# Folded score triangles and a three-operation rotary in a two-layer hybrid decoder kernel

## The chip, the cores and the metric

One core of a Trainium2 chip runs the whole program. Its engines work beside each other, each through its own instructions in order: TensorE (PE: matmuls and transposes into PSUM), VectorE (DVE), ScalarE (ACT), GpSimd (POOL) and the DMA queues, issued by SyncE (SP). The metric is the device time of one execution in microseconds; the median of several runs is compared.

## The reference, cut to what matters

Each of two layers normalises x, projects it to queries, keys, values and pooling channels, mixes tokens, projects back, and runs a SwiGLU network. All of it is float32. What the change touches is partial rotary and the sliding-window attention with sinks: 1024 positions, 8 query heads on 2 key heads of 64 channels, blocks of 128 positions, a window of 128.

```python
def partial_rotary(t, positions):          # first 16 of 64 channels of each head
    t1, t2, rest = tf[..., :half], tf[..., half:ROT_DIM], tf[..., ROT_DIM:]
    rot = jnp.concatenate([t1 * cos - t2 * sin, t2 * cos + t1 * sin, rest], axis=-1)
...
    scores = scores * (HEAD_DIM ** -0.5)   # queries of a block x (block before, own block)
    diff = qi + BLOCK - kj
    valid = (diff[None] >= 0) & (diff[None] < WINDOW) & (key_abs >= 0)
    scores = jnp.where(valid[None, :, None, None], scores, NEG_INF)
    probs = jax.nn.softmax(jnp.concatenate([scores, sink], axis=-1), axis=-1)[..., :-1]
    out = jnp.einsum("bnkgqs,bnskd->bnqkgd", probs.astype(v.dtype), v_cat)
```

With the window as wide as a block, query i of a block sees the keys j <= i of its own block and the keys j > i of the block before: two triangles that fill one 128 x 128 square between them.

## The kernel before

Every float32 product is computed as three matmuls (`mm3`, lines 263, 266, 267) on operands split into a high and a low part: ScalarE casts the high part (L220), VectorE subtracts it from the source (L221). Positions are worked in two halves of 512. For each layer and half, dense projections accumulate in four PSUM banks, and a weight's split is asked for one step ahead.

Attention is a generator of steps (`attention`, L940) that advances beside the dense steps (`run`, L693): 37 attention steps beside 20 dense steps for half 0 (L1490); for half 1, 16 beside the output projection of half 0 (L1496), 10 beside the pooling projection (L1521), and the rest beside the first gate/up products (L1525). A group is one block and one key head with its four query heads: 8 groups a half, 32 over both layers. Its steps are: rotary and keys (for the first key head of a block) and queries; softmax of the group before; scores of two heads and probabilities of the group before; the same for the other two heads. A group's value products are issued one step after its probabilities were transposed.

The generators set priorities; a scheduler at build time then orders each engine's instructions by priority and readiness, so that dense matmuls and attention matmuls mix on TensorE.

In a group, `att_scores` (L858) multiplies into one PSUM bank for two heads, [head, block before | own block]; VectorE adds the mask, takes the maximum and writes to SBUF (L869). `att_softmax` (L876) makes exponentials with a sum (L888), adds the sink's, and scales three heads on VectorE (L894) and one on ScalarE (L896). `att_probs` (L898) transposes 4 tiles for two heads (L904) and splits them (L220, L221); `att_values` (L913) multiplies 256 columns at a time. In block 0 there is no block before, and the tiles are half as wide. `att_rotary` (L787) has six VectorE instructions of 80 elements per block. Its tables are made at the start (L196 to L206) by a chain of small VectorE instructions.

Of the kernel before, what the change touches and what calls it, by code (L numbers as in the profile page):

```python
# [11 lines left out]
F32 = mybir.dt.float32  # L12
F32R = mybir.dt.float32r
# [7 lines left out]
P = 128  # L21
# [45 lines left out]
def hybrid_decoder_kernel(  # L67
# [70 lines left out]
    def msc_bank():  # L138
# [19 lines left out]
    pick_row = t_("rt", [P, 7])  # L158
# [29 lines left out]
    cos_t = const.tile([P, NB, RH], F32, name="cos_t")  # L188
    sin_t = const.tile([P, NB, RH], F32, name="sin_t")
# [5 lines left out]
    def rotary_angles():  # L195
# [591 lines left out]
    def att_rotary(blk, qkv):  # L787
        rot = qkv[:, 0:QK].rearrange("p (n d) -> p n d", d=HD)
        t1 = rot[:, :, 0:RH]
        t2 = rot[:, :, RH:ROT]  # L790
        nr = NH + NKV
        cb = cos_t[:, blk : blk + 1, :].to_broadcast([P, nr, RH])
        sbc = sin_t[:, blk : blk + 1, :].to_broadcast([P, nr, RH])
        tmp = t_("rt", [P, 4, nr, RH])
        nc.vector.tensor_mul(tmp[:, 0], t1, cb)
        nc.vector.tensor_mul(tmp[:, 1], t2, sbc)
        nc.vector.tensor_mul(tmp[:, 2], t2, cb)
        nc.vector.tensor_mul(tmp[:, 3], t1, sbc)
        nc.vector.tensor_sub(t1, tmp[:, 0], tmp[:, 1])
        nc.vector.tensor_add(t2, tmp[:, 2], tmp[:, 3])  # L800
# [57 lines left out]
    def att_scores(blk, n, u, qT, mx, s):  # L858

        kT = attn["k", blk]  # L860
        bank = msc_bank()
        cs = att_seen(blk)
        for ii in range(2):
            dst = bank[:, ii * 2 * P : (ii + 1) * 2 * P][:, cs]
            q = qT[:, (2 * u + ii) * P : (2 * u + ii + 1) * P]
            nc.tensor.matmul(dst, q, kT[:, 2 * n, cs], start=True, stop=False)
            nc.tensor.matmul(dst, q, kT[:, 2 * n + 1, cs], start=False, stop=True)
        for ii in range(2):
            nc.vector.tensor_tensor_reduce(  # L869
                out=s[:, ii, cs], in0=bank[:, ii * 2 * P : (ii + 1) * 2 * P][:, cs],  # L870
                in1=mask[:, cs], scale=SCALE, scalar=-3.0e38, op0=ALU.add, op1=ALU.max,
                accum_out=mx[:, 2 * u + ii : 2 * u + ii + 1],
            )
        return s

    def att_softmax(blk, n, sts, mx, nsink):  # L876
        hs = slice(n * GRP, (n + 1) * GRP)
        nm = t_("st", [P, 8])[:, :GRP]
        es = t_("st", [P, 8])[:, :GRP]
        sm = t_("st", [P, 8])[:, :GRP]  # L880
        nc.vector.scalar_tensor_tensor(
            nm, mx[:, :GRP], -1.0, nsink[:, hs], op0=ALU.mult, op1=ALU.min
        )
        nc.vector.tensor_sub(es, nm, nsink[:, hs])
        nc.scalar.activation(es, es, AF.Exp)
        for i in range(GRP):
            sl = sts[i // 2][:, i % 2, att_seen(blk)]
            nc.scalar.activation(sl, sl, AF.Exp, bias=nm[:, i : i + 1], accum_out=sm[:, i : i + 1])  # L888
        nc.vector.tensor_add(es, es, sm)
        nc.vector.reciprocal(es, es)  # L890
        for i in range(GRP):
            sl = sts[i // 2][:, i % 2, att_seen(blk)]
            if i < GRP - 1:
                nc.vector.tensor_scalar(sl, sl, es[:, i : i + 1], None, op0=ALU.mult)  # L894
            else:
                nc.scalar.activation(sl, sl, AF.Copy, scale=es[:, i : i + 1])  # L896

    def att_probs(blk, s):  # L898

        bank = msc_bank()  # L900
        for ck in range(0 if blk else 1, 2):
            for ii in range(2):
                i = 2 * ck + ii
                nc.tensor.transpose(  # L904
                    bank[:, i * P : (i + 1) * P], s[:, ii, ck * P : (ck + 1) * P], ident
                )
        ph = t_("pth", [P, 512], F32R)
        pl = t_("ph", [P, 512], F32R)
        cs = slice(0 if blk else 2 * P, 4 * P)
        split(ph[:, cs], pl[:, cs], bank[:, cs])  # L910
        return ph, pl

    def att_values(blk, n, u, probs, cat, t):  # L913
# [747 lines left out]
```

## Time and profile before

| | us |
|---|---|
| runs, median of 3 | 1906.67 |
| lowest, highest | 1903.42, 1907.11 |
| the profiled execution, first to last instruction (span) | 1904.4 |
| TensorE, VectorE, ScalarE, GpSimd busy in it | 1864.7, 1540.4, 948.4, 20.0 |

The profile gives the span as the profiled execution's own time; it lies 2.3 us under the median and inside the runs' range. Matmuls are pipelined: the record of a 512-column matmul lasts 0.39 us while the next one starts 0.227 us after it, so "busy" of TensorE says that work is in flight, and the distance between two starts says what an instruction costs. An idle time stands in brackets with the instruction that ended it.

### The profile page before, as it was taken

The page shows a single profiled execution, that of the slowest core. Times are in us where ns is not written, and L with a number is a line of the kernel's source. Part 1 is how long each engine was busy: PE and PEld are TensorE (multiplying, and loading weights), DVE is VectorE, ACT ScalarE, POOL GpSimd, SP SyncE. Part 2 cuts the span into 40 slices and gives each one's busy share as a digit, 9 for nine tenths or more (in the row PEclk, how much of TensorE's full clock was granted, in tenths as well). Part 3 has the DMA queues.
Part 4 walks back from the last instruction along what each step waited for, and adds up shares of the span by engine and source line. Part 5 has one row for each costly group of instructions (what it writes and reads, how often), then busy time and mean ns, then how long its engine had stood idle before and what let it go on. Part 6 is the DMA issues. An engine that isn't in the chain of part 4 may idle for free.

```text
span 1904.4 us, 26019 instructions
## 1 busy us (share of the span) xinstructions
PE 1864.7 (98%) x8954; PEld 1540.3 (81%) x8954; DVE 1540.4 (81%) x2889; ACT 948.4 (50%) x1791; POOL 20.0 (1%) x67
## 2 busy tenths in 40 slices
PE   7999999999999999999999999999999999999998
PEld 5887788888888788888888868888887888888886
DVE  7899886668898888788879988846888888867687
ACT  4875795654222223445558667845622222234452
POOL 0000000000000000000000000000000000000000
PEclk9999999999999999999999989999999999999999
DMA  9345563655555665944554464536654565574343
GB/s 341 112 144 161 161 221 125 191 172 193 194 183 188 205 210 172 320 143 150 172 179 139 126 181 164 178 111 209 214 189 146 198 216 197 199 249 157 117 141 114
DMA packets 229540, 341.86 MB, mean 180 GB/s; under 512 B 17016, under 2 KB 126472, under 8 KB 229408
## 3 DMA queue, kind: packets, MB, share of 16 engines
q1 hardware_dynamic: 228800, 338.10, 53.8%
q10 hardware_dynamic: 576, 2.10, 0.3%
q8 instruction: 70, 1.15, 0.3%
q14 instruction: 62, 0.51, 0.1%
q0 software_dynamic: 32, 0.00, 0.0%
HBM read 267.25 MB, written 72.89 MB: 179 GB/s over the span
## 4 chain that ended last, share of the span: by engine, by line
PE 80%; DVE 10%; DMA 5%; ACT 3%; issue 2%; SPq 0%; DVEq 0%; ACTq 0%; POOL 0%; POOLq 0%
PE acc L263 25%; PE acc L266 24%; PE acc L267 24%; DMA ar<-in_ada_w_dram 2%; DVE lo L221 1%; DVE ada L298 1%; DMA raw<-in_w_up_dram 1%; PE msc L904 1%; PE msc L561 1%; ACT hi L220 1%; PE pv L263 1%; PE pv L266 1%; PE pv L267 1%; ACT raw L554 1%; DVE fn L1162 1%
## 5 line engine op out<-in xcount | busy, mean ns | idle before, releaser
L220 ACT ACTIVATE hi<-raw 128x1024 fp32r<-128x1024 f32 (+1 forms) x388 | 331.8, 868 | 360.1 <-PE acc L266 197.1
L221 DVE TENSOR_TENSOR lo<-raw,hi 128x1024 fp32r<-128x1024 f32 (+1 forms) x388 | 380.2, 987 | 121.3 <-ACT hi L220 116.4
L263 PE MATMUL acc<-t,hi 128*128 128x512 f32 x704 | 274.6, 390 | 2.7 <-ACT hi L220 2.6
L266 PE MATMUL acc<-t,hi 128*128 128x512 f32 x704 | 274.0, 389 | 0.0
L267 PE MATMUL acc<-t,lo 128*128 128x512 f32 x704 | 271.8, 389 | 0.0
L263 PE MATMUL acc<-bh,hi 128*128 128x512 f32 x520 | 202.8, 390 | 0.0
L267 PE MATMUL acc<-bh,lo 128*128 128x512 f32 x520 | 202.4, 389 | 0.0
L263 PE MATMUL acc<-hT,hi 128*128 128x512 f32 x480 | 190.2, 396 | 0.6 <-DVE fn L691 0.6
L266 PE MATMUL acc<-hT,hi 128*128 128x512 f32 x480 | 188.4, 392 | 0.0
L267 PE MATMUL acc<-hT,lo 128*128 128x512 f32 x480 | 187.6, 392 | 0.0
L1162 DVE TENSOR_TENSOR fn<-acc,fn 128x512 f32<-128x512 f32 x220 | 150.3, 685 | 38.2 <-PE acc L267 37.6
L263 PEld LDWEIGHTS acc<-t,hi 128*128 128x128 f32 x704 | 132.2, 188 | 32.1 <-ACT hi L220 5.1
L267 PEld LDWEIGHTS acc<-t,lo 128*128 128x128 f32 x704 | 132.2, 188 | 28.7 <-DVE lo L221 1.2
L266 PEld LDWEIGHTS acc<-t,hi 128*128 128x128 f32 x704 | 132.2, 188 | 27.1
L266 PE MATMUL acc<-ph,hi 128*128 128x512 f32 x320 | 124.7, 390 | 0.0
L1098 ACT ACTIVATE fn<-fn 128x512 f32<-128x512 f32 x44 | 27.9, 633 | 181.7 <-DVE fn L1162 181.7
L263 PEld LDWEIGHTS acc<-bh,hi 128*128 128x128 f32 x520 | 97.6, 188 | 20.2
L267 PEld LDWEIGHTS acc<-bh,lo 128*128 128x128 f32 x520 | 97.6, 188 | 20.2
L298 DVE SCALAR_TENSOR_TENSOR ada<-ar,c_act,ada 128x512 f32<-128x512 f32 x140 | 104.6, 747 | 10.1 <-DMA ar<-in_ada_w_dram 9.7
L263 PE MATMUL acc<-hi 128*128 128x512 f32 x256 | 103.5, 410 | 2.4 <-DVE fn L691 2.0
L263 PEld LDWEIGHTS acc<-hT,hi 128*128 128x128 f32 x480 | 90.2, 188 | 19.2 <-DVE fn L691 1.4
L267 PEld LDWEIGHTS acc<-hT,lo 128*128 128x128 f32 x480 | 90.1, 188 | 18.6 <-issue 0.2
(323 smaller groups left out, 3814.5 us busy)
## 6 DMA issues: line engine op xcount, KB each, us to landing
ar<-in_ada_w_dram SPq DMA_DIRECT2D x160, 256.0 KB
raw<-in_w_gate_dram SPq DMA_DIRECT2D x44, 512.0 KB
raw<-in_w_up_dram SPq DMA_DIRECT2D x44, 512.0 KB
raw<-in_w_in_dram SPq DMA_DIRECT2D x80, 256.0 KB
raw<-keeps SPq DMA_DIRECT2D x40, 512.0 KB
keeps<-fn SPq DMA_DIRECT2D x66, 256.0 KB
two_b<-in_w_down_dram SPq DMA_DIRECT2D x30, 512.0 KB
raw<-keepa SPq DMA_DIRECT2D x25, 512.0 KB
```

Of the source, the lines that this page charges most:

```text
L220: a = nc.scalar.activation(hi, src, AF.Copy)
L221: v = nc.vector.tensor_sub(lo, src, hi.bitcast(F32))
L263: ins = nc.tensor.matmul(dst, lh, rh, start=first, stop=False)
L266: nc.tensor.matmul(dst, lh, rl, start=False, stop=False)
L267: return nc.tensor.matmul(dst, ll, rh, start=False, stop=last)
L298: ins = nc.vector.scalar_tensor_tensor(acc, w, c_act[:, i : i + 1], acc, op0=ALU.mult, op1=ALU.add)
L554: nc.scalar.activation(hf, bank, AF.Identity, bias=shift, scale=scale)
L561: ins = nc.tensor.transpose(bank[:, t * P : (t + 1) * P], src[t], ident)
L904: nc.tensor.transpose(bank[:, i * P : (i + 1) * P], s[:, ii, ck * P : (ck + 1) * P], ident)
L1098: nc.scalar.activation(g, g, AF.Silu)
L1162: nc.vector.tensor_add(halves_of(dst)[m], bank, halves_of(src)[m])
```

## The change

The scores of both triangles are folded into one tile S of [128, 4 heads, 128 + 1]. ScalarE copies the block before from PSUM to S, VectorE copies the own block over it where key j <= query i (a predicated copy with the mask `own`), and the 129th column holds the sink divided by the scale, copied there by GpSimd. One maximum over 129 columns and one negated scaling follow; the exponentials run over 129 columns, and their sum includes the sink. One multiplication scales all four heads. Four transposes and one split per group follow; then GpSimd cuts the triangles apart again, in the transposed tiles: two selects write the own block's part (`here`), two clear it from the other (`seen`). In block 0 GpSimd fills S with a large negative number in place of ScalarE's copy, and there are two selects. Value products take all four heads at once, the own block first; they are issued after the next group's queries, three steps after the transposes. Rotary works on both halves at once, with a table of (-sin, sin) and one of (cos, cos), and its scratch is the rest of S's tile. The mask table becomes 128 wide; `pth` has four buffers in place of two, `st` nine in place of twelve.

```diff
-    SMALL = dict(junk=1, st=12, rs=8, ss=4, halo=8, rows=1, cols=2, colp=4, sk=2)
+    SMALL = dict(junk=1, st=9, rs=8, ss=4, halo=8, rows=1, cols=2, colp=4, sk=2)
-        mix=dict(cfa=2, cfb=2, qkv=5, bqkv=1, uT=4, pt=2, vz=5, rt=1, qT=1, pth=2, pwh=1, pwl=1),
+        mix=dict(cfa=2, cfb=2, qkv=5, bqkv=1, uT=4, pt=2, vz=5, qT=1, pth=4, pwh=1, pwl=1),
...
-    mask = const.tile([P, 2 * P], F32, name="mask")
-    nc.gpsimd.memset(mask, 0.0)
-    fill = NEG / SCALE
+    own = const.tile([P, P], F32, name="own")
+    nc.gpsimd.memset(own, 1.0)
     nc.gpsimd.affine_select(
-        out=mask, in_=mask, pattern=[[-1, 2 * P]], compare_op=ALU.is_ge,
-        fill=fill, base=P, channel_multiplier=1,
-    )
-    nc.gpsimd.affine_select(
-        out=mask, in_=mask, pattern=[[1, 2 * P]], compare_op=ALU.is_gt,
-        fill=fill, base=0, channel_multiplier=-1,
+        out=own, in_=own, pattern=[[-1, P]], compare_op=ALU.is_ge,
+        fill=0.0, base=0, channel_multiplier=1,
     )
...
-    cos_t = const.tile([P, NB, RH], F32, name="cos_t")
-    sin_t = const.tile([P, NB, RH], F32, name="sin_t")
+    cos_t = const.tile([P, NB, ROT], F32, name="cos_t")
+    sin_t = const.tile([P, NB, ROT], F32, name="sin_t")
...
-        nc.vector.tensor_scalar(sin_t, ang, math.pi, -math.pi, op0=ALU.min, op1=ALU.max)
-        nc.vector.scalar_tensor_tensor(cos_t, sin_t, -1.0, sin_t, op0=ALU.mult, op1=ALU.max)
-        nc.vector.tensor_scalar(cos_t, cos_t, -1.0, math.pi / 2.0, op0=ALU.mult, op1=ALU.add)
+        halves = [slice(0, RH), slice(RH, ROT)]
+        up = sin_t[:, :, halves[1]]
+        nc.vector.tensor_scalar(up, ang, math.pi, -math.pi, op0=ALU.min, op1=ALU.max)
+        nc.vector.tensor_scalar(sin_t[:, :, halves[0]], up, -1.0, None, op0=ALU.mult)
+        nc.vector.tensor_tensor(turns, sin_t[:, :, halves[0]], up, op=ALU.max)
+        for half in halves:
+            nc.vector.tensor_scalar(cos_t[:, :, half], turns, -1.0, math.pi / 2.0, op0=ALU.mult, op1=ALU.add)
...
+    def att_rotary(blk, qkv, room):
         rot = qkv[:, 0:QK].rearrange("p (n d) -> p n d", d=HD)
...
+        both = rot[:, :, 0:ROT].rearrange("p n (o d) -> p n o d", o=2)
         nr = NH + NKV
...
+        cb, sbc = (
+            tab[:, blk : blk + 1, :].rearrange("p b (o d) -> p b o d", o=2).to_broadcast([P, nr, 2, RH])
+            for tab in (cos_t, sin_t)
+        )
+        tmp = room[:, : 2 * nr * RH].rearrange("p (n o d) -> p n o d", n=nr, o=2)
+        nc.vector.tensor_mul(tmp, both[:, :, ::-1, :], sbc)
+        nc.vector.tensor_mul(both, both, cb)
+        nc.vector.tensor_add(both, both, tmp)
...
+    def att_scores(blk, u, qT, kT, S):
         bank = msc_bank()
         cs = att_seen(blk)
         for ii in range(2):
             dst = bank[:, ii * 2 * P : (ii + 1) * 2 * P][:, cs]
             q = qT[:, (2 * u + ii) * P : (2 * u + ii + 1) * P]
...
+            nc.tensor.matmul(dst, q, kT[0][:, cs], start=True, stop=False)
+            nc.tensor.matmul(dst, q, kT[1][:, cs], start=False, stop=True)
+        both = bank.rearrange("p (i o k) -> p i o k", i=2, o=2)
+        dst = S[:, 2 * u : 2 * u + 2, 0:P]
+        if blk:
+            nc.scalar.activation(dst, both[:, :, 0, :], AF.Copy)
+        else:
+            nc.gpsimd.memset(dst, NEG)
+        seen = own.bitcast(I32).rearrange("p (o k) -> p o k", o=1).to_broadcast([P, 2, P])
+        nc.vector.copy_predicated(dst, seen, both[:, :, 1, :])
+    def att_max(S):
+        mx = t_("st", [P, 8])[:, :GRP]
+        nc.vector.tensor_reduce(mx, S, axis=mybir.AxisListType.X, op=ALU.max)
+        nc.vector.tensor_scalar(mx, mx, -SCALE, None, op0=ALU.mult)
+        return mx
+    def att_softmax(S, nm):
+        sm = t_("st", [P, 8])[:, :GRP]
+        es = t_("st", [P, 8])[:, :GRP]
+        for i in range(GRP):
+            nc.scalar.activation(
+                S[:, i, :], S[:, i, :], AF.Exp, bias=nm[:, i : i + 1], scale=SCALE, accum_out=sm[:, i : i + 1]
             )
...
+        nc.vector.reciprocal(es, sm)
+        nc.vector.tensor_mul(
+            S[:, :, 0:P], S[:, :, 0:P], es.rearrange("p (i o) -> p i o", o=1).to_broadcast([P, GRP, P])
         )
...
+    def att_probs(blk, S):
+        bank = msc_bank()
         for i in range(GRP):
...
+            nc.tensor.transpose(bank[:, i * P : (i + 1) * P], S[:, i, 0:P], ident)
+        seen = [t_("pth", [P, 512], F32R) for _ in range(2)]
+        split(*seen, bank)
+        views = [r.rearrange("p (i q) -> p i q", i=GRP) for r in seen]
+        if not blk:
+            for v in views:
+                nc.gpsimd.affine_select(
+                    out=v, in_=v, pattern=[[0, GRP], [1, P]], compare_op=ALU.is_ge,
+                    fill=0.0, base=0, channel_multiplier=-1,
                 )
...
+            return [None, seen]
+        here = [t_("pth", [P, 512], F32R) for _ in range(2)]
+        for v, r in zip(views, here):
+            nc.gpsimd.affine_select(
+                out=r.rearrange("p (i q) -> p i q", i=GRP), in_=v, pattern=[[0, GRP], [1, P]],
+                compare_op=ALU.is_ge, fill=0.0, base=0, channel_multiplier=-1,
+            )
+        for v in views:
+            nc.gpsimd.affine_select(
+                out=v, in_=v, pattern=[[0, GRP], [-1, P]], compare_op=ALU.is_gt,
+                fill=0.0, base=0, channel_multiplier=1,
+            )
+        return [seen, here]
+    def att_values(blk, n, probs, cat, t):
+        if n == 0:
             attn["pv"] = ps.tile([P, 512], F32, tag="pv", name="pv", bufs=1)
         pv = attn["pv"]
...
+        for ck in (1, 0) if blk else (1,):
             vh, vl = attn["v", blk - 1 + ck]
             vs = slice(n, n + 2)
...
+            opening = n == 0 and ck == 1
+            closing = n == NKV - 1 and ck == (0 if blk else 1)
             ins = mm3(
...
+                pv, vh[:, vs].rearrange("p a d -> p (a d)"), vl[:, vs].rearrange("p a d -> p (a d)"),
+                *probs[ck], opening, closing, None if opening else attn["open"],
             )
             if opening:
                 attn["open"] = ins
...
+        if n == NKV - 1:
             nc.scalar.activation(
                 cat[:, :, t * P : (t + 1) * P], pv.rearrange("p (j q) -> p j q", j=GRP), AF.Copy
             )
...
+    def attention(h, qkvs, sink, cat):
         NG = NT * NKV
         prev, late = None, []
             if g < NG:
                 t, n = divmod(g, NKV)
                 blk = h * NT + t
+                both = t_("sb", [P, D])
+                S = both[:, : GRP * (P + 1)].rearrange("p (i k) -> p i k", i=GRP)
+                room = both[:, GRP * (P + 1) :]
                 if n == 0:
                     if t == 0:
...
+                        att_rotary(blk, qkvs[t], room)
                     att_keys(blk, qkvs[t])
                     if t + 1 < NT:
...
+                        att_rotary(blk + 1, qkvs[t + 1], room)
                 qT = att_queries(n, qkvs[t])
...
+                hs = slice(n * GRP, (n + 1) * GRP)
+                nc.gpsimd.tensor_copy(S[:, :, P : P + 1], sink[:, hs].rearrange("p (i o) -> p i o", o=1))
                 yield
+            flush()
             if prev:
...
+                att_softmax(prev[3], prev[4])
                 yield
             for u in range(GRP // 2):
+                if cur is None and g < NG:
+                    cur = (blk, n, t, S)
                 if cur:
+                    kT = attn["k", blk]
+                    att_scores(blk, u, qT, (kT[:, 2 * n], kT[:, 2 * n + 1]), S)
+                    if u:
+                        cur = (*cur, att_max(S))
+                if prev and u == 0:
+                    late.append((prev[0], prev[1], att_probs(prev[0], prev[3]), cat, prev[2]))
                 yield
+        nc.vector.tensor_scalar(sk, sk, 1.0 / SCALE, None, op0=ALU.mult)
+        d["bq"], d["sink"] = bq, sk
```

## Rows read from the trace of the kernel before

**Rows 1.** The page's head and first part: busy us, share of the span, instructions.

```profile
span 1904.4 us, 26019 instructions
PE 1864.7 (98%) x8954; PEld 1540.3 (81%) x8954; DVE 1540.4 (81%) x2889; ACT 948.4 (50%) x1791; POOL 20.0 (1%) x67
```

**Rows 2.** Table by stage: busy us (instructions) of each engine, clock, DMA share, GB/s.

```profile
60.00:160.00 100.00, 98.36 (x622) 85.06 (x621) 93.76 (x288) 77.01 (x194) 3.33 (x11) 1.00 0.40 122
160.00:205.00 45.00, 40.38 (x184) 30.72 (x183) 40.31 (x103) 28.02 (x67) 0.28 (x1) 0.92 0.62 180
450.00:500.00 50.00, 50.00 (x222) 41.41 (x221) 39.52 (x51) 11.55 (x13) 0.00 (x0) 1.00 0.52 169
1000.00:1096.00 96.00, 94.36 (x592) 81.27 (x592) 90.40 (x276) 74.29 (x188) 3.59 (x11) 1.00 0.44 133
...
165.40:168.80 3.40, 3.27 (x12) 2.33 (x11) 3.40 (x7) 3.03 (x6) 0.00 (x0) 0.50 0.56 154
1131.40:1138.20 6.80, 6.24 (x13) 4.37 (x14) 6.59 (x19) 3.32 (x11) 0.70 (x1) 0.50 0.59 164
```

**Rows 3.** TensorE's waits over the span: us in total, times, longest.

```profile
PE msc L332 <- DVE ident L152: 11.2, 1, 11.2
PE msc L904 <- DVE sb L894: 2.1, 5, 0.6
PE pv L263 <- ACT pth L220: 1.8, 2, 0.9
```

**Rows 4.** Timeline of TensorE, 263.5 to 268.2 us: start, us, instruction [idle before].

```profile
...
263.89 0.28 PE L267 MATMUL pv<-pth,vz 128*128 128x256 f32 x1
264.01 0.60 PE L904 MATMUL msc<-ident,sb 128*128 128x128 f32 x4
264.45 0.60 PE L561 MATMUL msc<-ident,fn 128*128 128x128 f32 x4
...
266.44 0.39 PE L263 MATMUL pv<-pth,vz 128*128 128x256 f32 x1 [0.92 <-ACT pth L220]
```

**Rows 5.** Groups by line, VectorE: out<-in, shape, xcount, busy, mean ns.

```profile
L869 DVE CUSTOM_DVE_ANT_0 sb<-msc,mask 128x256 f32<-128x256 f32 x112 | 44.2, 416 | 7.8 <-PE msc L867 7.4
L869 DVE DVE_READ_ACCUMULATOR2_ANT st<- 128x1 f32 x128 | 10.4, 82 | 0.0
L894 DVE TENSOR_SCALAR sb<-sb,st 128x256 f32<-128x256 f32 x84 | 24.5, 346 | 0.3
L221 DVE TENSOR_TENSOR ph<-msc,pth 128x512 fp32r<-128x512 f32 x56 | 38.2, 685 | 1.3 <-issue 0.4 <-ACT pth L220 0.4
L881 DVE SCALAR_TENSOR_TENSOR st<-st,sk 128x4 f32<-128x4 f32 x32 | 5.0, 155 | 0.1
L796 DVE TENSOR_TENSOR rt<-qkv,sin_t 128x80 f32<-128x80 f32 x16 | 3.8, 235 | 0.0
```

**Rows 6.** Groups by line, ScalarE.

```profile
L888 ACT ACTIVATE sb<-sb,st 128x256 f32<-128x256 f32 x112 | 55.6, 502 | 5.9 <-DVE st L881 5.9
L888 ACT ACTIVATION_READ_ACCUMULATOR sb<-sb,st 128x1 f32 x128 | 24.7, 193 | 0.0
L220 ACT ACTIVATE pth<-msc 128x512 fp32r<-128x512 f32 x56 | 33.0, 597 | 20.7 <-PE msc L904 20.6
```

**Rows 7.** GpSimd: two groups by line, and its timeline from 955 to 958 us.

```profile
L166 POOL TENSOR_SCALAR_AFFINE_SELECT mask<-mask 128x256 f32<-128x256 f32 x1 | 0.4, 391 | 0.0
masks.py:199 POOL TENSOR_SCALAR_AFFINE_SELECT G<-G 128x128 f32<-128x128 f32 x1 | 0.3, 299 | 0.1
...
955.25 2.24 POOL L808 CAST vz<-vz_zero 128x64 fp32r<-128x64 f32 x4 [680.14 <-ACT hT L220]
957.48 0.23 POOL L808 CAST vz<-vz_zero 128x64 fp32r<-128x64 f32 x1
```

**Rows 8.** Timeline of VectorE, 10.3 to 11.7 us.

```profile
...
10.84 0.20 DVE L206 TENSOR_SCALAR cos_t<-cos_t 128x64 f32<-128x64 f32 x1
10.95 0.22 DVE L152 CAST ident<-G 128x128 fp32r<-128x128 f32 x1
```

More of the change, by code (lines that the diff above doesn't have):

```diff
@@ L157, in hybrid_decoder_kernel @@
     ones = ones_r.bitcast(F32)
-    pick_row = t_("rt", [P, 7])
+    pick_row = t_("pth", [P, 7])
     nc.vector.memset(pick_row, 0.0)
@@ L865, in att_scores @@
             q = qT[:, (2 * u + ii) * P : (2 * u + ii + 1) * P]
[L866 to L872, printed above, removed]
-            )
@@ L874, in att_scores @@
[L874 to L882, printed above, removed]
-        )
-        nc.vector.tensor_sub(es, nm, nsink[:, hs])
-        nc.scalar.activation(es, es, AF.Exp)
+            nc.tensor.matmul(dst, q, kT[0][:, cs], start=True, stop=False)
@@ L886, in att_softmax @@
         for i in range(GRP):
[L887 to L905, printed above, removed]
-                )
[L907 to L911, printed above, removed]
@@ L913, in att_values @@
-    def att_values(blk, n, u, probs, cat, t):
-        if n == 0 and u == 0:
+            nc.tensor.transpose(bank[:, i * P : (i + 1) * P], S[:, i, 0:P], ident)
[7 more added lines that the diff above has]
+                    fill=0.0, base=0, channel_multiplier=-1,
+                )
+            return [None, seen]
@@ L916, in att_values @@
+        return [seen, here]
+    def att_values(blk, n, probs, cat, t):
+        if n == 0:
             attn["pv"] = ps.tile([P, 512], F32, tag="pv", name="pv", bufs=1)
         pv = attn["pv"]
-        ph, pl = probs
-        first = 0 if blk else 1
-        for ck in range(first, 2):
+        for ck in (1, 0) if blk else (1,):
             vh, vl = attn["v", blk - 1 + ck]
             vs = slice(n, n + 2)
-            cs = slice(ck * 2 * P, (ck + 1) * 2 * P)
-            opening = n == 0 and u == 0 and ck == first
-            closing = n == NKV - 1 and u == 1 and ck == 1
+            opening = n == 0 and ck == 1
+            closing = n == NKV - 1 and ck == (0 if blk else 1)
@@ L926, in att_values @@
             ins = mm3(
-                pv[:, u * 2 * P : (u + 1) * 2 * P],
-                vh[:, vs].rearrange("p a d -> p (a d)"), vl[:, vs].rearrange("p a d -> p (a d)"),
-                ph[:, cs], pl[:, cs], opening, closing, None if opening else attn["open"],
+                pv, vh[:, vs].rearrange("p a d -> p (a d)"), vl[:, vs].rearrange("p a d -> p (a d)"),
+                *probs[ck], opening, closing, None if opening else attn["open"],
             )
@@ L932, in att_values @@
                 attn["open"] = ins
-        if closing:
+        if n == NKV - 1:
             nc.scalar.activation(
@@ L938, in hybrid_decoder_kernel @@
     ATT_STEPS = NT * NKV * 4 + 3
-    def attention(h, qkvs, nsink, cat):
+    def attention(h, qkvs, sink, cat):
         NG = NT * NKV
@@ L1370, in layer_rows @@
         eng.dma_start(sk, sinks[l : l + 1, :].to_broadcast([P, NH]))
-        nc.vector.tensor_scalar(sk, sk, -1.0, None, op0=ALU.mult)
-        d["bq"], d["nsink"] = bq, sk
+        nc.vector.tensor_scalar(sk, sk, 1.0 / SCALE, None, op0=ALU.mult)
+        d["bq"], d["sink"] = bq, sk
     rows0 = load_col_rows(0)
@@ L1477, in hybrid_decoder_kernel @@
         qkvs[1] = [t_("qkv", [P, QKV]) for _ in range(NT)]
-        att = attention(0, qkvs[0], par["nsink"], cats[0][0])
+        att = attention(0, qkvs[0], par["sink"], cats[0][0])
         def dense():
@@ L1494, in hybrid_decoder_kernel @@
         fn, ss, out0 = mix_out(l, cats[0], G)
-        att = attention(1, qkvs[1], par["nsink"], cats[1][0])
+        att = attention(1, qkvs[1], par["sink"], cats[1][0])
         run(out0, 2 * KD, (side, 4 * ADA), (att, 16))
```

24 lines of the change are left out of this document (removed).

## Prediction, made before the change was built

> **What bounds the kernel now.** I read the engine shares first, then a table by stage, then TensorE's waits, and only then the single instructions. TensorE is busy for 1864.7 of 1904.4 us [rows 1]. Its matmuls overlap in the records, so "busy" also covers short waits; the distance between starts tells more. A stage without attention has 222 matmuls in 50 us, 0.225 us per 512 columns [rows 2], with nothing lost between them. The attention stages are 60 to 160 us (layer 0, half 0) and 1000 to 1096 us (layer 1), where TensorE is busy 98.4 of 100 and 94.4 of 96 us while VectorE is at 93.8 and 90.4 [rows 2]: two engines are near full there, and TensorE is the fuller one. In 160 to 205 us TensorE is busy 40.4 of 45 us at a mean clock of 0.92, and in 1131.4 to 1138.2 us it ran at 0.50 [rows 2], that is 1.2 instead of 2.4 GHz.
>
> In the list of TensorE's waits the attention chain itself holds little: 2.1 us for the probabilities that VectorE scales (L894) and 1.8 us for their high halves (L220) [rows 3]. So work taken off VectorE and ScalarE can give back about 4 us by itself; work taken off TensorE counts almost in full.
>
> **TensorE's part.** There are 32 groups (2 layers, 8 blocks, 2 key heads); the first block's 4 groups see no earlier block. Before, a group transposes 8 probability tiles (4 in the first block): 28 x 8 + 4 x 4 = 240. After, both triangles lie in one tile, so it is 4 always: 128. That removes 112. Four of them start at 264.01 and the next work at 264.45, 0.11 us each [rows 4]: 112 x 0.11 = 12.3 us. The value products keep their columns but are issued 512 wide: before 28 x 12 + 4 x 6 = 360 of 256 columns at 0.12 us (263.89 to 264.01, [rows 4]), 43.2 us; after 28 x 6 + 4 x 3 = 180 at 0.225, 40.5 us: 2.7 us less. Scores and the transposes of queries and keys stay. Sum: -15.0 us, all of it in stages where TensorE starts work after work; about 32 of the 112 transposes (3.5 us) fall in the less full stages at 160 to 205 and 1096 to 1140 us, which is the soft part of this term.
>
> **VectorE's part.** A group before: four score reductions (0.416) with four accumulator reads (0.082), four small ones of about 0.16, three scalings (0.346), two subtractions of 512 (0.685) [rows 5]: 1.66 + 0.33 + 0.64 + 1.04 + 1.37 = 5.04 us. After: two predicated copies of 256 out of PSUM, a maximum over 4 x 129, two small ones, one broadcast multiplication of 512 and one subtraction of 512. Predicated copies are not in this trace: between a small one (0.155) and a 512 subtraction (0.685), I take the score reduction's 0.416, which has the same size and source. The maximum is between 0.155 and two passes of 0.685; I take 0.69, as for 512 elements. 0.83 + 0.69 + 0.33 + 0.685 + 0.685 = 3.22 us, 1.8 less, 28 times: -51 us; the first block's groups, 128 wide before, give about 2 more. Rotary: six at 0.235 [rows 5] become three of double width, between 0.235 and 0.416; at 0.32, 1.41 becomes 0.96, 16 times: -7 us. VectorE loses about 60 of its busy time. Hidden behind TensorE, that is worth nothing by itself; what it can return is a share of the 3.9 us in [rows 3]. I take 2 us; the ends are 0 and 3.9.
>
> **ScalarE's part.** Four exponentials of 256 (0.502) become 129 wide, one of two casts (0.597) goes, and two copies out of PSUM come [rows 6]. The exponentials save at most half, 4 x 0.25 = 1.0; the copies cost between 0.193 and 0.597 each, say 0.4, so that they eat the cast and a little more: about -0.9 us a group with the scaled copy and the sink's exponential that also go, some 25 us, covered by TensorE as well. But the copy is a new link: VectorE's predicated copy writes over the same tile and waits for it, and behind that wait stand VectorE's weight splits, for which the dense matmuls wait. Its price is between 0 and one exponential in front of it (0.5 us) a group, 16 us in all; I take nothing, since VectorE has just gained 1.8 us a group.
>
> **GpSimd's part.** The triangles are cut out after the transposition: four selects of 512 elements a group (two in the first block), 28 x 4 + 4 x 2 = 120, and the values wait for them. The trace has selects of 128 and 256 elements, 0.299 and 0.391 us [rows 7]; a straight line through them gives 0.575 for 512, an estimate. Then 69 us on an engine that has 20 us of work: no limit by throughput. But it's latency: ScalarE's cast (0.6) and then four in a row, 2.9 us from transposes to the last operand. They may also run slower beside VectorE: four casts of 64 elements took 2.24 us while VectorE subtracted, 0.56 each, against 0.23 for one begun while VectorE was idle (957.48) [rows 7]. With 0.33 us more each the chain is 4.2 us.
> The Trainium skill ("SBUF — State Buffer", section "Who interferes with whom") says that a VectorE instruction with two SBUF inputs and a GpSimd instruction that reads SBUF exclude each other for the whole instruction. The slow casts agree with it; that VectorE is held up too, no row here shows. By that rule 120 selects would block VectorE for up to 69 us, more than the 60 saved, and the sum would be about 10 us less good wherever VectorE then sets the pace.
>
> What covers the latency: in half 0, 37 attention steps run beside 20 dense steps of 12 matmuls (2.7 us); probabilities are transposed in a group's third step and used three steps later, with one dense step between in five of eight groups and two in three. One dense step plus the next scores and queries (about 0.8 us) is 3.5 us, and the later operands are needed up to 0.9 us after the first. That covers 2.9 and about covers 4.2. The cover is thin at the end of half 1, where the last attention steps are emitted in one bunch with the gate/up products: today TensorE waits 0.92 us there for the cast [rows 4]. There are two such places a layer, four in all, each at 0 (dense matmuls put in front) to 4.2 us. I take 1.0 each: +4 us.
>
> **Start.** The tables of doubled width need five VectorE instructions in place of three, and the identity matrix, for which TensorE's first instruction waits 11.2 us [rows 3], is converted right behind them: the next starts 0.11 to 0.25 us later [rows 8]. Two more are +0.45 us (ends 0 and 0.6).
>
> **Sum.** -15.0 - 2 + 4 + 0.45 = -12.5, so a span of 1891.9 us. The span of before lies 2.3 us under the median of its runs (1906.67); with that, 1894.2 us. Less than 0.2% (3.8 us) is no change that a measurement of this kernel can tell: faster is under 1902.9, slower over 1910.5.
>
> **Rivals.**
> 1. VectorE was the hidden limit. Then its 60 us less also removes the waits of [rows 3] and the half-clock stretches that follow idle time (four in the layers' attention stages, of 3.4 to 6.8 us, the first and the longest in [rows 2]; 17 us at 0.50 together, which cost 8.5). 1904.4 - 15.0 + 0.45 - 3.9 - 8.5 = 1877.5, with 2.3 us 1880. For it: VectorE at 94%. Against it: TensorE has almost no waits on it. Chance 0.12.
> 2. The bunches at the end of half 1 cost their upper end, 4 x 4.2 = 16.8 us, and eat the gain: 1904.4 - 15.0 + 0.45 + 16.8 = 1906.7, with 2.3 us 1909. For it: TensorE waits there today. Against it: the order on TensorE mixes dense work in between (L561 stands between L904 and L866 in [rows 4]). Chance 0.13.
> 3. The other side: GpSimd's four selects become the last link of every value step, because each must wait for VectorE's two-input instructions, and TensorE, which works in order, stands at the values. It decides from 14.5 / 32 = 0.45 us a group on. At 1.0 us a group it is +32: 1904.4 - 14.5 + 32 = 1921.9, with 2.3 us 1924. For it: the slow casts, and the single dense step. The skill's rule on the port would be its mechanism. Against it: 3.5 to 4.4 us of cover against 2.9 to 4.2. Chance 0.12.
> 4. The edit doesn't relieve VectorE: predicated copy and maximum at their upper ends (2 x 0.27 + 0.68 = 1.2 us more a group) and, should the hold-up that the casts of [rows 7] show also work the other way, VectorE stands for every select: -60 + 28 x 1.2 + 69 = +43 us. Half the groups, with 21 us, run in 60 to 160 and 1000 to 1096 us, where VectorE has 6.2 + 5.6 us free [rows 2]; about 10 us of dense work come late. 1891.9 + 10 + 2.3 = 1904. For it: how full VectorE is. Against it: both copies and maximum would have to be far from the rows nearest to them. Chance 0.08.
> My forecast has 0.55, with a range of its own of 1887 to 1902.
>
> **How the numbers follow.** Faster: 0.55 + 0.12 + 0.07 from rivals 2 and 4 short of their ends = 0.74. Slower: rival 3 and 0.01 of rival 2, 0.13. Same: the rest, 0.13. The range reaches from rival 1 to rival 2: 1880 to 1909; outside it lie rival 3 and the low tail.
>
> **What would show it.** Right: 128 probability transposes and 180 value products at 0.225 us; VectorE's busy time near 1480 us and ScalarE's near 925; TensorE's first instruction at about 11.7 us; 120 selects near 0.6 us; value products that wait for GpSimd at a few places only. Wrong: selects over 1 us, a row in TensorE's waits in which the value products wait for GpSimd for over 10 us, or VectorE's weight splits waiting behind a predicated copy; more half-clock stretches than the few of now.

## The result, and the profile after

The changed kernel takes 1911.26 us (median of 20 runs, 1907.95 to 1917.38), the kernel before beside it 1907.76 us (20 runs): a ratio of 1.0021, with a 95% interval of 1.0014 to 1.0028. It is slower by some 3.5 us, 0.2%, about the least that these runs can tell from no change. The forecast of 1894.2 us and its range up to 1909 are both missed.

First the page's head after, for [rows 1]; columns as there.

```profile
span 1908.4 us, 25284 instructions
PE 1852.8 (97%) x8662; PEld 1515.1 (79%) x8662; DVE 1529.4 (80%) x2523; ACT 924.2 (48%) x1755; POOL 129.6 (7%) x226
```

TensorE has 292 instructions and 11.9 us of busy time less, and yet the span is 4.0 us longer. VectorE gave up 366 instructions but only 11 us of busy time, where the forecast has 60. ScalarE is where it was forecast (925). GpSimd has 110 us more, where 69 were estimated.

The table by stage after, for [rows 2]; 205 to 300 us holds the end of half 1. The last three are all the half-clock stretches of the attention stages.

```profile
60.00:160.00 100.00, 95.60 (x546) 78.88 (x545) 91.04 (x194) 68.27 (x178) 29.68 (x49) 1.00 0.41 125
160.00:205.00 45.00, 40.77 (x197) 32.02 (x196) 40.97 (x81) 28.89 (x74) 4.57 (x8) 0.96 0.57 169
205.00:300.00 95.00, 88.92 (x440) 71.29 (x439) 78.59 (x154) 72.33 (x171) 26.66 (x40) 0.98 0.58 191
1000.00:1096.00 96.00, 91.76 (x530) 75.65 (x528) 86.50 (x183) 67.08 (x176) 28.08 (x51) 1.00 0.44 133
...
167.70:171.10 3.40, 3.40 (x13) 2.74 (x13) 3.40 (x8) 3.23 (x7) 0.00 (x0) 0.50 0.51 130
266.60:270.00 3.40, 3.40 (x10) 2.63 (x9) 3.27 (x4) 2.77 (x5) 3.40 (x4) 0.51 0.96 296
1106.30:1109.70 3.40, 3.40 (x9) 2.61 (x9) 3.40 (x7) 2.15 (x4) 0.00 (x0) 0.50 0.39 106
```

From 60 to 160 us TensorE is now busy 95.60 us, against 98.36 [rows 2]: where it was all but full, it stands idle. The clock is not the reason: three stretches at 0.50, 10.2 us, against four with 17 us before. Counted at half their length, as the prediction does, they cost 5 us against 8.5, so the clock gave some 3 us back (an estimate).

TensorE's waits after, for [rows 3] (us in total, times, longest):

```profile
PE msc L331 <- DVE ident L152: 11.3, 1, 11.3
PE msc L822 <- DVE hi L817: 3.8, 2, 2.6
PE acc L262 <- ACT hi L219: 3.6, 3, 1.7
PE acc L262 <- DVE fn L690: 3.3, 5, 1.8
PE msc L843 <- DVE hi L840: 3.2, 5, 0.9
...
PE pv L265 <- POOL pth L913: 2.6, 5, 0.8
...
PE msc L895 <- DVE sb L887: 1.9, 4, 0.6
PE pv L262 <- POOL pth L913: 1.7, 6, 0.3
```

The value products wait for GpSimd for 5.1 us over all rows of this view, close to the 4 forecast. More is lost to VectorE: without the start, its rows sum to 18.0 us, against 10.1 before and 10.7 in the changed kernel without its selects (below). TensorE's stalls can be followed better in a ledger: for each matmul the distance from its start to the next start, summed by what the matmul is. Besides the transposes of probabilities and the value products it has one more column, for all other matmuls; it covers the time from the first matmul to the last.

| us | transposes of probabilities | value products | everything else | first start |
|---|---|---|---|---|
| before | 22.9 (x240) | 49.3 (x360) | 1812.0 | 11.2 |
| after | 12.6 (x128) | 51.3 (x180) | 1824.3 | 11.3 |
| difference | -10.3 | +2.0 | +12.2 | +0.1 |

Everything else is the same work in both kernels, and it takes 12.2 us longer, although the clock fell less often. That is the loss to be explained.

### The profile page after: what moved, and what is told of

It reads as the page before. It is cut to its first block, busy times and chain, and to the rows that moved or that the text cites. A ratio compares the mean times of both kernels' runs of the same rounds, so it can differ in the third digit from the quotient of the medians.

```text
span 1908.4 us, 25284 instructions
## 1 busy us (share of the span) xinstructions
PE 1852.8 (97%) x8662; PEld 1515.1 (79%) x8662; DVE 1529.4 (80%) x2523; ACT 924.2 (48%) x1755; POOL 129.6 (7%) x226
## 4 chain that ended last, share of the span: by engine, by line
PE 71%; DVE 14%; DMA 6%; ACT 4%; issue 3%; POOL 1%; SPq 1%; POOLq 0%; DVEq 0%; ACTq 0%
PE acc L262 22%; PE acc L265 22%; PE acc L266 22%; DMA ar<-in_ada_w_dram 3%; DVE lo L220 2%; DVE ada L297 2%; DMA raw<-in_w_up_dram 1%; ACT hi L219 1%; PE msc L560 1%; DMA ar<-x 1%; POOL pth L913 1%; DVE fn L1171 1%; DVE pth L220 1%; DMA raw<-in_w_in_dram 0%; DVE sb L871 0%
## 5 line engine op out<-in xcount | busy, mean ns | idle before, releaser
L220 DVE TENSOR_TENSOR lo<-raw,hi 128x1024 fp32r<-128x1024 f32 (+1 forms) x388 | 384.0, 997 | 122.8 <-ACT hi L219 120.3
L297 DVE SCALAR_TENSOR_TENSOR ada<-ar,c_act,ada 128x512 f32<-128x512 f32 x140 | 108.6, 776 | 9.1 <-DMA ar<-in_ada_w_dram 8.4
L266 PEld LDWEIGHTS acc<-bh,lo 128*128 128x128 f32 x520 | 97.6, 188 | 20.4
```

The source lines that it names most:

```text
L220: v = nc.vector.tensor_sub(lo, src, hi.bitcast(F32))
L266: return nc.tensor.matmul(dst, ll, rh, start=False, stop=last)
L297: ins = nc.vector.scalar_tensor_tensor(acc, w, c_act[:, i : i + 1], acc, op0=ALU.mult, op1=ALU.add)
```

## Experiments

All ratios are to the kernel before, run on the same chip, with 95% intervals. Theory: the selects cost the gain, by holding VectorE up, by standing ahead of the values, or both. Rivals: the rotary, the fold itself, the order of the program.

**Selects left out.**

```diff
-        here = [t_("pth", [P, 512], F32R) for _ in range(2)]
-        for v, r in zip(views, here):
-            nc.gpsimd.affine_select(...)
...
-        return [seen, here]
+        return [seen, seen]
```

> Leaves out GpSimd's 120 selects: the value products of both blocks read the one uncut tile of probabilities, so the triangles are not cut apart. Theory A (the selects are what eats TensorE's saving: 4.8 us of TensorE waiting for them, and about 24 us by which VectorE's two-input instructions beside them got longer): 12 to 17 us under the changed kernel, ratio to before about 0.993 to 0.995. Theory B (the folded order itself, with a maximum and a multiplication of 512 in one piece, makes the other work late, selects or not): at most the 5 us of direct waits, ratio 0.999 to 1.000. Theory C (rotary and its longer start are the loss): at most 5 us as well.

Measured: 1888.23 us, 0.9887 (0.987 to 0.9904). The selects turn a gain of about 21.5 us into a loss of about 4 (by the ratios; the medians of this run and its own kernel before differ by 20.4). In the ledger: transposes 12.7, values 46.1, everything else 1807.4. The first two are -13.4 against before, near the 15.0 forecast, and everything else is 4.6 less. That much can be the clock alone: without the selects only two stretches, 6.8 us, are left at 0.50, which by the same count is worth 5 us against before.

```profile
164.30:167.70 3.40, 3.40 (x11) 2.72 (x10) 3.40 (x7) 2.69 (x6) 0.00 (x0) 0.50 0.46 141
526.10:529.50 3.40, 3.40 (x10) 2.20 (x9) 3.40 (x4) 1.01 (x2) 0.00 (x0) 0.50 0.09 29
```

VectorE's groups show what the selects do to it. By line, first without the selects, then in the changed kernel (mean ns behind the busy time):

```profile
L297 DVE SCALAR_TENSOR_TENSOR ada<-ar,c_act,ada 128x512 f32<-128x512 f32 x140 | 104.5, 746 | 10.2 <-DMA ar<-in_ada_w_dram 9.3
...
L220 DVE TENSOR_TENSOR pth<-msc,pth 128x512 fp32r<-128x512 f32 x32 | 22.0, 687 | 3.3 <-ACT pth L219 3.0
...
L220 DVE TENSOR_TENSOR hT<-raw,hT 128x512 fp32r<-128x512 f32 x32 | 21.5, 686 | 13.5 <-ACT hT L219 13.5
...
L993 DVE TENSOR_TENSOR pt<-uT 128x527 f32<-128x527 f32 x16 | 11.2, 701 | 0.5
```

```profile
L297 DVE SCALAR_TENSOR_TENSOR ada<-ar,c_act,ada 128x512 f32<-128x512 f32 x140 | 108.6, 776 | 9.1 <-DMA ar<-in_ada_w_dram 8.4
...
L871 DVE COPY_PREDICATED sb<-own,msc 128x256 f32<-128x256 int32 x64 | 28.5, 445 | 6.9 <-ACT sb L867 6.9
...
L220 DVE TENSOR_TENSOR hT<-raw,hT 128x512 fp32r<-128x512 f32 x32 | 23.5, 750 | 13.1 <-ACT hT L219 13.1
...
L220 DVE TENSOR_TENSOR pth<-msc,pth 128x512 fp32r<-128x512 f32 x32 | 22.0, 688 | 4.2 <-ACT pth L219 3.8
L887 DVE TENSOR_TENSOR sb<-sb,st 128x512 f32<-128x512 f32 x32 | 21.9, 685 | 0.3
L875 DVE TENSOR_REDUCE st<-sb 128x4 f32<-128x516 f32 x32 | 21.8, 683 | 0.3
...
L1011 DVE TENSOR_TENSOR pt<-uT 128x527 f32<-128x527 f32 x16 | 12.6, 787 | 0.5
...
L795 DVE TENSOR_TENSOR sb<-qkv,sin_t 128x160 f32<-128x160 f32 x16 | 5.9, 371 | 0.2 <-PE msc L895 0.2
```

Instructions that read two tiles in SBUF grew (hT 686 to 750, pt 701 to 787, ada 746 to 776 ns); the subtraction of the same size with one input in PSUM (pth<-msc,pth) did not, 687 and 688. These means hide how much one instruction grows. In the changed kernel's trace hT takes 1024 ns in the six cases with a select beside it and 686 in the other 26; ada 942 (21 cases) and 747 (119); the subtraction out of PSUM 688 either way (26 and 6). The multiplication sb<-sb,st reads SBUF twice too, but no select ever runs beside it. Over all of VectorE the durations sum to 22.1 us more with the selects (1682.2 against 1660.1). Where a bunch of selects meets such instructions, both slow down. The changed kernel's timelines of VectorE and of GpSimd (start in us, duration in us, instruction):

```profile
288.49 0.69 DVE L1011 TENSOR_TENSOR pt<-pt 128x521 f32<-128x521 f32 x1
289.22 1.00 DVE L1015 SCALAR_TENSOR_TENSOR pt<-pt,uT 128x512 f32<-128x512 f32 x1
290.14 1.65 DVE L220 TENSOR_TENSOR lo<-raw,hi 128x1024 fp32r<-128x1024 f32 x1
291.72 1.13 DVE L1011 TENSOR_TENSOR pt<-uT 128x527 f32<-128x527 f32 x1
```

```profile
287.92 1.76 POOL L908 TENSOR_SCALAR_AFFINE_SELECT pth<-pth 128x512 fp32r<-128x512 f32 x2 [5.41 <-ACT pth L219]
289.64 2.65 POOL L913 TENSOR_SCALAR_AFFINE_SELECT pth<-pth 128x512 fp32r<-128x512 f32 x2
```

VectorE's 1.65 us stands against a mean of 1.225 for that split in the changed kernel, the 1.13 against 0.701, and the last two selects take 1.32 us each.

The Trainium skill ("SBUF — State Buffer", section "Who interferes with whom") says that a VectorE instruction with two inputs in SBUF and a GpSimd instruction that reads SBUF shut each other out, and that one that only writes does not. The two forms of L220 agree (750 against 688 ns); the writing side is tested next.

**Selects that nobody reads, smaller ones, and fills in their place.** The values read the uncut tiles; GpSimd works beside them, and nobody reads what it writes.

```diff
# 120 selects of 512 columns into scratch
+        for v, r in zip(views, outs):
+            nc.gpsimd.affine_select(out=r, in_=v, ...)
-        return [seen, here]
+        return [seen, seen]
# as many, of 128 columns
+        outs = [r.rearrange("p (i q) -> p i q", i=GRP)[:, 0:1] for r in here]
+        views = [v[:, 0:1] for v in views]
# as many fills of 512 columns
+        for r in here * (2 if blk else 1):
+            nc.gpsimd.memset(r.bitcast(F32), 0.0)
```

> All 120 selects stay on GpSimd and read the same tiles, but write to two tiles that nobody reads; the value products read the uncut tile and do not wait for them (the triangles are not cut apart). It keeps what the selects do to VectorE and takes away their place in the chain. Theory A1 (VectorE held up beside the selects): within 3 us of the changed kernel, ratio 1.000 to 1.002. Theory A2 (latency before the value products): as without selects, ratio 0.993 to 0.996.

> As the run with unread selects, but each of the 120 reads and writes 128 columns (one head) in place of 512, about 0.3 in place of 0.58 us alone. If VectorE is held for as long as a select lasts, the price over no selects falls from 13 us to about 6 us: 1893 to 1896 us. If the price is one per instruction, 1899 to 1903 us. If it was only the order, anything.

> As the run with unread selects, but each of the 120 selects is a memset of the same 512 columns: GpSimd is busy and writes, but reads nothing (the triangles are not cut apart). Theory A1 (VectorE's two-input instructions are held while GpSimd reads): VectorE's subtractions back at 0.687 us and the time as without selects, 1886 to 1892 us, ratio 0.988 to 0.991. If any GpSimd work, or only another order of the instructions, cost the 13 us: 1898 to 1903 us.

Measured: unread selects 1901.51 us, 0.9958 (0.9944 to 0.9972); small ones 1891.99, 0.9918 (0.9903 to 0.9933); fills 1890.36, 0.9919 (0.9905 to 0.9934). By the ratios, unread selects cost 13.5 of the 25 us just by being there. Fills and small selects cost some 6 us over no selects; the other 7.5 go when GpSimd reads nothing, or a quarter. Two lines of VectorE with unread selects, and one with fills:

```profile
L297 DVE SCALAR_TENSOR_TENSOR ada<-ar,c_act,ada 128x512 f32<-128x512 f32 x140 | 106.1, 758 | 11.7 <-DMA ar<-in_ada_w_dram 11.1
L220 DVE TENSOR_TENSOR hT<-raw,hT 128x512 fp32r<-128x512 f32 x32 | 23.8, 760 | 12.7 <-ACT hT L219 12.4
```

```profile
L297 DVE SCALAR_TENSOR_TENSOR ada<-ar,c_act,ada 128x512 f32<-128x512 f32 x140 | 104.2, 745 | 9.5 <-DMA ar<-in_ada_w_dram 8.7
```

With a fill beside it, ada has 745 ns (13 cases), as without one; beside an unread select 834 (19). No fill ran beside an hT in this run; in the run with three fills a tile (below) ten did, at 686 ns.

**A chain without the hold.** In place, and read by the values: two selects of 128 columns a group; two fills of each tile; three fills of each. The fills leave zeros where the probabilities stood.

```diff
+            nc.gpsimd.affine_select(out=v[:, 0:1], in_=v[:, 0:1], ...)
+        return [seen, seen]
# fills, two rounds (one in block 0); then 3 and 2
+        for _ in range(2 if blk else 1):
+            for r in seen:
+                nc.gpsimd.memset(r.bitcast(F32), 0.0)
+        return [seen, seen]
```

> The changed kernel, but each of the two probability tiles of a group is cut in place on 128 of its 512 columns only (64 selects of 128 columns), and both value products read that tile. The output is therefore not the reference's. GpSimd stands between split and values again, with a short chain (two selects of 0.38 to 0.41 us as in e9, against four of 0.74 to 0.86 us, 3.2 us in all), and the hold on VectorE is as small as in e9 (1891.99 us). Theory A (the other 12 us of the selects are the chain's length, in proportion): 1892 + 12 x 0.8/3.2 = about 1895 us. Theory B (any operation of GpSimd ahead of the values costs them, short or long, by the order and the hand-over): about 1904 us. Theory C (the chain costs only where the selects also hold VectorE up): 1892 us, as e9.

> The changed kernel, but in place of the selects GpSimd fills the split probability tiles with zeros, two fills of 512 columns for each tile (one in block 0), 120 fills ahead of the values, which read those tiles. The attention's values are therefore zeros and the output not the reference's. The fills read nothing, so by e5 they hold VectorE up by nothing (1890.36 us when nobody waits for them), and take 0.52 us each, 2.1 us a group ahead of the values against 3.2 us of the selects. Theory A (the chain's length, in proportion): 1890 + 12 x 2.1/3.2 = about 1898 us. Theory B (any operation ahead of the values): about 1902 us. Theory C (chain costs only together with the hold on VectorE): 1890 us.

> As e11 (zeros in place of the probabilities, so the output is not the reference's), with three fills of each tile instead of two (two in block 0): 176 fills of 0.53 us, 3.2 us a group ahead of the values, as long as the four selects of the changed kernel. Theory A (the chain's length, with slack for 2.1 us that 3.2 us oversteps): about 1890 + 12 = 1902 us. Theory C (a chain of this length costs nothing by itself; what the selects cost comes of their hold on VectorE, which makes the splits late that the chain starts from): 1890 to 1894 us.

Measured: 1890.77 us, 0.9904 (0.989 to 0.9919); 1893.57, 0.9917 (0.9902 to 0.9931); 1890.14, 0.9908 (0.9892 to 0.9924). Theory C (a chain costs only beside the hold on VectorE) fits each time: a chain as long as that of the selects costs nothing that these intervals show against the unread fills (0.9905 to 0.9934). GpSimd by line in the last one, and TensorE's wait on it:

```profile
L901 POOL MEMSET pth<- 128x512 f32 x184 | 89.2, 533 | 68.1 <-DVE pth L220 67.1 <-DVE rs L280 1.0
```

```profile
PE pv L262 <- POOL pth L901: 1.2, 3, 0.5
```

Six fills of 0.533 us stand ahead of a group's values (four in block 0; 184 in all, not the 176 expected), 3.2 us, and TensorE waits 1.2 us for them in the whole run. So the cover that the prediction counted (3.5 to 4.4 us) is there.

The changed kernel's chain is as long and stands at the same place, but it reads: 1.0021 against 0.9908, some 21 us. It also takes four `pth` tiles a group in place of two. The trace shows no wait from that: ScalarE's cast into them waits for the transposes (18.4 us in all in the changed kernel, 19.8 with three fills), never for a value product.

**Half the chain, all of the hold.** The two clearing selects stand ahead of the values; the other two write tiles that nobody reads.

```diff
-        return [seen, here]
+        return [seen, seen]        # and the two selects of `seen` first
```

> The changed kernel with all its 120 selects, but per group only the two that clear the block before stand ahead of the values; both value products read their tiles, and the two selects of the own block write tiles that nobody reads. One triangle is therefore missing and the output not the reference's. Hold on VectorE as in the changed kernel and in e2; chain of 1.6 us against 3.2 and 0. Theory C (a chain costs only beside the hold, in proportion): about 1907 us, between e2 (1901.5) and the changed kernel (1911.3). If the chain costs only when all four selects are in it: 1902 us. If being behind any long select costs the whole: 1911 us.

Measured: 1912.97 us, 1.0027 (1.0014 to 1.004). Half of the chain beside the whole hold costs as much as the changed kernel, not half; the proportion that I had expected is refuted. In the ledger the values take 48.4 us, everything else 1832.5. TensorE's waits with unread selects, then with half the chain:

```profile
PE acc L262 <- DVE fn L690: 3.2, 5, 1.6
PE msc L560 <- DVE fn L540: 2.9, 2, 1.4
PE msc L843 <- DVE hi L840: 2.0, 4, 1.2
...
PE msc L895 <- DVE sb L887: 1.8, 5, 0.4
```

```profile
PE msc L560 <- DVE fn L540: 4.4, 3, 1.7
...
PE msc L843 <- DVE hi L840: 3.8, 6, 1.4
PE msc L895 <- DVE sb L887: 3.1, 5, 1.0
...
PE acc L262 <- DVE fn L690: 3.1, 4, 1.8
...
PE pv L265 <- POOL pth L907: 2.7, 8, 0.4
PE msc L843 <- DVE sb L871: 2.5, 2, 2.1
PE pv L262 <- POOL pth L907: 1.9, 5, 0.6
```

GpSimd is waited for about as long as in the changed kernel (4.6 us over all rows); what grew is the waiting for VectorE, from 20.3 over all rows (its start's wait is named by a DMA) to 25.3 without the start. Part of the difference is the clock: this run's trace has five stretches at 0.50, 20.5 us together (168.2 to 175.0 is the longest), against 6.8 with unread selects. At half their length that is some 7 of the 10.8 us by which everything else is longer here (1821.7 there).

**The two halves of the edit.** The fold with the old rotary and tables; the kernel before with the new ones.

```diff
# fold only: six operations, tables of single width
+        nc.vector.tensor_mul(tmp[:, 0], t1, cb)
...
# rotary only, in the kernel before
+        nc.vector.tensor_mul(tmp, both[:, :, ::-1, :], sbc)
...
```

> The folded triangles with the rotary and the tables of before (six instructions per block, scratch in the same room). Theory C (rotary and its longer start cost 1 to 2 us): ratio 1.001, 1 to 2 us under the changed kernel. If rotary in three operations is worth what was forecast (some 7 us of VectorE that nobody waits for): same as the changed kernel but for the start, 0.5 us.

> The kernel of before with rotary in three operations on the doubled tables, and nothing folded. Theory C: +1 to +1.5 us, all of it at the start where two more small VectorE instructions stand ahead of the identity, ratio 1.0005 to 1.001. If the shorter rotary relieves VectorE: 0.998 to 0.9995.

Measured: fold only 1912.04 us, 1.0013 (1.0 to 1.0026); rotary only 1907.03, 0.9992 (0.9982 to 1.0003). The fold with its selects is the whole change; the rotary moves nothing that these runs can tell.

**Fewer selects, and none.** With the own block's cut tile multiplied by (own values - values before), and the uncut tile by the values before, the clearing selects can go: 64 in place of 120, for two subtractions and one split more a block (two scratch buffers, `UW` and `halo`, are made smaller for the differences). The second kernel cuts that one triangle on VectorE, with the old rotary.

```diff
+            for v in attn["v", blk - 1]:
+                nc.vector.tensor_sub(vsrc, vsrc, v[:, 0:3:2, :].bitcast(F32))
...
-        for v in views:
-            nc.gpsimd.affine_select(out=v, in_=v, pattern=[[0, GRP], [-1, P]], ...)
...
-            vh, vl = attn["v", blk - 1 + ck]
+            vh, vl = attn["d", blk] if blk and ck else attn["v", blk - 1 + ck]
# second kernel, for the remaining selects
+            nc.vector.tensor_mul(r.rearrange("p (i q) -> p i q", i=GRP), v.bitcast(F32), keep)
```

> The changed kernel with half the selects: the uncut probabilities multiply the values of the block before, and the own block's triangle multiplies the difference of both blocks' values, so that nothing is cleared from the first tile. 64 selects in place of 120, the first three value matmuls need none, and VectorE gets three small instructions per block more. Theory A: half of the 13 us for VectorE and over half of the 12 us of latency go, 4 us come back for the small instructions: 1896 to 1902 us, ratio 0.993 to 0.997, faster than both kernels. Theory B: no gain, 1908 or more.

> The same with differences of values, but VectorE cuts the own triangle by two multiplications with a mask (0.61 us from start to start each, 34 us of VectorE in all), no selects, and rotary as before. VectorE is then about as full as before the change, and TensorE's saving of 15 us stays: 1890 to 1898 us, ratio 0.991 to 0.996. If 34 us more of VectorE cost as much as the selects did (20 us of VectorE for 13 us of time): 1908 or more.

Measured: 64 selects 1901.19 us, 0.9973 (0.9964 to 0.9982), faster than the kernel before and, in the same terms, than the changed one (1.0021, 1.0014 to 1.0028). Cut on VectorE: 1922.65 us, 1.0081 (1.0067 to 1.0094), the slowest of all, without a select in a group. The work moved to VectorE costs more than the selects did: its page has VectorE at 1555.4 us, 47 above the kernel without selects, and the time is some 37 us longer by the ratios. The expected 1890 to 1898 us is missed; its other branch, 1908 or more, is what came.

Over the folded kernels, which all have 8662 matmuls and transposes on TensorE, its time for everything else (by the ledger) follows VectorE's busy time on the whole, whatever fills that; of two kernels with the same busy time one can still lie 6 us above the other:

| kernel | VectorE busy, us | everything else on TensorE, us |
|---|---|---|
| no selects | 1508.2 | 1807.4 |
| fills, unread | 1508.1 | 1808.0 |
| small selects, unread | 1509.1 | 1814.3 |
| short chain | 1509.5 | 1813.6 |
| chain of two rounds of fills | 1510.7 | 1810.2 |
| chain of three rounds | 1510.6 | 1810.0 |
| 64 selects | 1525.5 | 1819.1 |
| selects, unread | 1527.7 | 1821.7 |
| changed kernel | 1529.4 | 1824.3 |
| fold with the old rotary | 1532.2 | 1821.4 |
| half the chain | 1536.3 | 1832.5 |
| cut on VectorE, no selects | 1555.4 | 1833.3 |

The kernels that aren't folded don't lie on this line: before, everything else takes 1812.0 us beside 1540.4 us of VectorE, and with the new rotary alone 1812.8 beside 1536.6. So VectorE's busy time explains the folded kernels among themselves. Why they pay more for the same busy time than the kernel before was not tested.

## Why the prediction was wrong, step by step

**What bounds the kernel: half right.** TensorE does start work after work, but VectorE at 94% [rows 2] was the nearer limit than its few waits in [rows 3] said. Those rows show what is late now, not how little is missing until more is late. In the kernel before, 32 us less of VectorE gave 4.6 us at most; in the folded one, 22 us more of it cost 17.

**TensorE's part: right.** Transposes -10.3 us against -12.3 (the mean of all is 0.095 us, not the 0.11 of one place). Value products without selects -3.2 against -2.7. The 180 have a median distance of 0.232 us.

**VectorE's part: the size failed.** 32 us of busy time went without selects (1540.4 to 1508.2), not 60. The durations were right or near (predicated copy 0.445 against 0.416, maximum 0.683 against 0.69, multiplication 0.685), and their sum falls by 58 us (1718.2 to 1660.1); but they are not what an instruction costs: VectorE's records overlap too, by some 0.08 us, and many small ones were removed. The kernel before's timeline of VectorE:

```profile
129.33 0.14 DVE L889 TENSOR_TENSOR st<-st 128x4 f32<-128x4 f32 x1
129.40 0.41 DVE L869 CUSTOM_DVE_ANT_0 sb<-msc,mask 128x256 f32<-128x256 f32 x1
129.74 0.07 DVE L869 DVE_READ_ACCUMULATOR2_ANT st<- 128x1 f32 x1
129.74 0.16 DVE L890 RECIPROCAL st<-st 128x4 f32<-128x4 f32 x1
129.83 0.38 DVE L869 CUSTOM_DVE_ANT_0 sb<-msc,mask 128x256 f32<-128x256 f32 x1
```

From start to start a small one is 0.07 to 0.09 us, and the accumulator read (0.082 in [rows 5]) is nothing: the next starts with it. The prediction said this of matmuls and didn't ask it of VectorE. That relief was worth at most 4.6 us of everything else on TensorE, where 2 was forecast, and the clock's share alone can be that much.

**GpSimd's part: the step that failed.** Its sum was "+4 us" for latency. That term was about right: values +2.0 us in the ledger against -2.7 + 4 = +1.3. What the sum left out is the hold of the selects on VectorE. The prediction told of it and put it at "about 10 us less good", but as "no row here shows" it, the sum has nothing for it. The runs show it, and it is larger: selects took 743 and 856 ns, not 575, and 22 us more of VectorE's durations; everything else on TensorE went from 1807.4 (no selects) to 1824.3 us. With -10.3, +2.0 and +0.1, the forecast's -2 of VectorE became +12.2.

**ScalarE's part and start: right.** 924.2 us against 925; the tables cost 0.1 us, inside 0 to 0.6.

**Rivals.** Rival 4 named the hold on VectorE, and with 1904 was on the wrong side of before: the selects put back 21 us of busy time (1508.2 to 1529.4), where it had 43 added to before; but each of those 21 costs more than the free time in [rows 2] allows for. Rival 3's end, slower, came true by another mechanism: TensorE stands 5.1 us, not 32, at the values. Rival 2: one bunch, in layer 0, has a half-clock stretch at 266.6 us; the waits are short. Rival 1 was right in part: without selects, 10 of the 17 us at half clock go, and everything else on TensorE is 4.6 us shorter; with the selects VectorE isn't relieved.

**Signs.** Most of the signs of being wrong didn't come, though the forecast was: selects stayed at 0.86 us, value products waited 5.1 us for GpSimd, and the half-clock stretches became fewer. They watched the chain and the clock. What told was VectorE's busy time, 1529.4 us where "near 1480" was forecast.

**What stays open.** Unread selects give 1901.5 us; read by the values, even two of four, 1911 to 1913. Chains of fills show that it is not latency by itself. TensorE's waits for VectorE don't say where the 10 us go: they grow with half the chain (20.3 to 25.3 us), but are 18.0 in the changed kernel. The build orders the instructions of these kernels differently, so how much of the 10 us is order, how much the clock, and how much the hold meeting the chain wasn't separated. Nor is it shown what the 6 us are that fills and small selects cost.

## What to carry to other kernels

When work goes from a full engine to an idle one, price what the idle one does to the full one, not only its own latency: here GpSimd had over 90% of its time free, a chain of 3.2 us of fills was covered, and the selects' reads of SBUF still cost more than the whole gain. Take savings on VectorE from the distances between starts, not from durations. If GpSimd must help beside a busy VectorE, let it write without reading, or read less: half the selects made this change a gain.

## What the runs showed of the hardware that was not expected

- A select of 128 x 512 takes 0.63 us at its fastest in the timelines read (103.47 us) and 1.32 in a bunch beside VectorE's two-input instructions; fills of the same size take 0.53 us and leave VectorE's two-input subtractions alone (686 ns beside a fill, 685 otherwise).
- Not only what reads two tiles in SBUF gets longer: a scaling of one tile (L295, ada<-ar,c_act, 128x512) takes 479 ns by itself, 688 in the mean of three cases beside a select, and, with three fills a tile, 814 in the mean of four beside a fill. A predicated copy out of PSUM takes 446 ns beside a select and 444 otherwise.
- Rotary's three operations of 160 elements take 0.317 to 0.321 us each in the run with the rotary alone, the six of 80 took 0.235 [rows 5]. VectorE's busy time falls by 3.8 us (1540.4 to 1536.6), half of what the durations promise, and the runs' times tell no difference.
